# Four attentions with unnormalised weights, head pairs scaled by rows spread by way of DRAM, token sums in two steps

## The chip, the cores and the metric

One core of a Trainium2 chip runs the whole program. The metric is device time in microseconds from start to end of one execution; three runs of the kernel before are shown, and one more execution was profiled. TensorE multiplies matrices (weights are loaded into its array, the other operand streams through, results go to PSUM); VectorE and ScalarE work on tiles element by element and read PSUM and SBUF; GpSimd works on SBUF alone; SyncE only issues transfers (DMA). Each engine takes its own instructions in a fixed order and waits on semaphores for the others.

## The reference, cut to what matters

512 tokens (16 more, called meta, in the first block) of width 1024 pass one block and then two layers.

- First block: a forgetting attention (8 heads of 64; scores plus a decay bias, causal) and a latent attention (8 heads, queries and keys of 96, values of 64, mask by chunks). Each: `p = softmax(s); out = p @ v`, then times a gate `silu(...)`; both join into `@ w_out`, a norm and a residual.
- Each of the two layers: four branches on the same normed input, a recurrent one (mLSTM, 4 heads of 128), a grouped-query attention (8 heads of 64 on 2 key heads), a neighbourhood attention (8 heads of 64, on windows of keys with a bias table) and a differential attention (4 heads with values of 128); each branch's output goes through an up-projection times a gate, the sum through `w_out`, then a feed-forward part `(silu(h @ w_gate) * (h @ w_up)) @ w_down` of width 2816.

A softmax row may be normalised before or after the product with v: `(e / sum) @ v = (e @ v) / sum`. The four attentions with heads of 64 values (forgetting, latent, grouped-query, neighbourhood) are those that the change touches.

## The kernel before, in words

All products run in fp32r with operands split in a high and a low part (`evict_split`, L208, from PSUM; `split_w`, L217, for weights), and three products hi*hi, hi*lo, lo*hi (`mm3`, L248). Weights stream in tiles of 512 KB, three deep (`raw`, L226), issued by SyncE and split by ScalarE (high) and GpSimd or VectorE (low) into tiles three deep.

TensorE's order is the program's (`manual_schedule`, L671). The order on the other engines and on SyncE's queue is written by the framework's planner, which simulates the program and takes what is ready first; after that it is fixed. Between the attentions' steps a stream of projections is run (`Stream`, L74; `overlap`, L129): each head and each tile of 128 queries is one map with four stages, score (0), transpose (1), product with v (2) and, for the last map of a pair, `done` (3). Scores run `look` maps ahead of the transposes; stages 2 and 3 follow the transposes by `lag` maps. The numbers stand in L33 to L37: forgetting attention 2 ahead, 2 and 3 behind; latent 3, 3 and 5; grouped-query 3, 3 and 4; neighbourhood 3, 2 and 4.

**Scores.** `softmax` (L330), `softmax_of_sum` (L338) and `softmax_banks` (L348) write exponentials to a tile `p`, sum them on the way and take the reciprocal; then the score stage multiplies `p` by it: L1019 (forgetting, VectorE), L1059 and L1061 (latent, ScalarE for odd and VectorE for even query tiles), L1696 (grouped-query) and L1779 (neighbourhood), both VectorE.

**Heads.** `Head.trans` (L416) transposes `p` by blocks of 128 on TensorE (L316) into a PSUM bank and splits it into `pth` and `ptl` (L211, L212). `Head.pv` (L438, every second query tile) multiplies with v. Its stationary operand holds v's high part in columns 0 to 63 and its low part in 64 to 127 (L453 to L455), so of a head's 512 tokens the result has 128 rows, of which row d and row d + 64 must be added. At the last tile ScalarE copies all 128 rows to SBUF (L458). `pair_out` (L460) joins two heads: two transfers within SBUF move halves to the other 64 partitions (L464, L465), two VectorE adds (L466, L467) give a tile with one head in rows 0 to 63 and the other in 64 to 127. `done` multiplies it by the gate and splits it for the next product. Four pairs in each of the first block's attentions and four in each layer's two make 24.

**The feed-forward entry.** `ffn` (L1148) makes its first pair of gate and up tiles with plain products (`pair`, L1179), later pairs with a scheme of seven products (`fast_pair`, L582), which needs sums of quarters of the tokens and of the weights. `Tokens.sums` (L563) makes the token sums: for each half of the rows four differences (L571 to L574) and four splits (L576, L577). It is called between the two gates and the two ups of the first pair. Every second weight tile of the later pairs goes into tiles of the tag `qs` (L1150), in which the token quarters lie until the sums have read them. The weight sums are L599 to L602, their splits L591 and L592.

Tiles of one tag share a few buffers: `t2` has six (L319), `yn` (`gate_tile`, L525) three, PSUM's `A` eight banks.

Of the kernel before, what the change touches and what calls it, by code (L numbers as in the profile page):

```python
# [14 lines left out]
ALU = mybir.AluOpType  # L15
# [3 lines left out]
P = 128  # L19
# [146 lines left out]
def hybrid_kernel(ctx: ExitStack, tc: tile.TileContext, i: dict, out: bass.AP):  # L166
# [162 lines left out]

    def softmax(src, dst):  # L330

        st = new(small, [P, 3], "sm")
        V.tensor_reduce(st[:, 0:1], src, AX.X, ALU.max, negate=True)
        A_.activation(dst, src, AF.Exp, bias=st[:, 0:1], accum_out=st[:, 1:2])
        V.reciprocal(st[:, 2:3], st[:, 1:2])
        return st[:, 1:2], st[:, 2:3]

    def softmax_of_sum(parts, dst, scale=-1.0):  # L338
# [6 lines left out]
        V.reciprocal(st[:, 3:4], st[:, 2:3])  # L345
        return st[:, 2:3], st[:, 3:4]

    def softmax_banks(parts, dst):  # L348

        if len(parts) == 1:  # L350
            return softmax(parts[0][0], dst)[1]
# [7 lines left out]
        V.reciprocal(st[:, 5:6], st[:, 5:6])  # L359
        return st[:, 5:6]  # L360

# [46 lines left out]
    class Head:  # L408
# [3 lines left out]

        def __init__(self, v, blocks, meta=None):
            self.v, self.blocks, self.meta, self.pt, self.pm = v, blocks, meta, {}, {}

        def trans(self, t, p, col):  # L416

            if t % 2 == 0:
                self.pt[t // 2] = [new(pool, [P, 4, 256], n, F32R) for n in ("pth", "ptl")]
                if self.meta:  # L420
                    k.pm_turn = 256 - k.pm_turn
                    self.pm[t // 2] = [a[:, k.pm_turn:k.pm_turn + 256] for a in k.pm]
            qs = slice((t % 2) * P, (t % 2 + 1) * P)
            bl = self.blocks(t)
            pt = bank()
            if self.meta:
                if t % 2 == 0:
                    self.pmt = bank()[0:NMETA, 0:256]
                transpose(self.pmt[:, qs], p[:, self.meta[1]:self.meta[1] + NMETA])
            for j, b in enumerate(bl):  # L430
                transpose(pt[:, j * P:(j + 1) * P], p[:, col(b):col(b) + P])
            src = pt[:, 0:len(bl) * P].rearrange("p (b q) -> p b q", q=P)
            sl = slice(bl[0], bl[-1] + 1)
            evict_split(src, *(a[:, sl, qs] for a in self.pt[t // 2]))
            if self.meta and t % 2:
                evict_split(self.pmt, *(a[0:NMETA] for a in self.pm[t // 2]))

        def pv(self, t):  # L438
# [17 lines left out]
            if t == 3:  # L456
                self.z = t2()
                A_.copy(self.z, self.ps)  # L458

    def pair_out(heads):  # L460

        a, b = (h.z for h in heads)
        e = t2()
        nc.sync.dma_start(e[0:64], a[64:128])  # L464
        nc.sync.dma_start(e[64:128], b[0:64])  # L465
        V.tensor_tensor(e[0:64], a[0:64], e[0:64], ALU.add)  # L466
        V.tensor_tensor(e[64:128], b[64:128], e[64:128], ALU.add)  # L467
        return e

# [87 lines left out]
    class Tokens:  # L557
# [5 lines left out]
        def sums(self):  # L563
# [5 lines left out]
            for c in (slice(0, 2), slice(2, 4)):  # L569
# [5 lines left out]
                for j in (1, 2, 0, 3):  # L575
                    A_.copy(self.t[j][0][:, c], t[j])  # L576
                    V.tensor_tensor(self.t[j][1][:, c], t[j], f(self.t[j][0][:, c]), ALU.subtract)  # L577

        def quarter(self, a, b):
# [148 lines left out]
def first_body(k, fb, col, hl):  # L728
# [75 lines left out]

    def head(hd, v, vm):
        return k.Head(lambda b: v[:, b, hd], lambda t: list(range(t + 1)), (vm[:, hd], 0))

# [197 lines left out]
    def fox_head(hd):  # L1005
        u, e = fox.units[hd // 2], hd % 2
        st = Work()
        hobj = head(hd, *fox.v)
        fox.heads[hd] = hobj

        def sc(t):
# [5 lines left out]

            r = k.softmax_of_sum([(sp, st.cb[:, a:b], a, b) for sp, a, b in sps], p)[1]
            V.tensor_scalar(p, p, r, None, ALU.mult)  # L1019
            if t == 3 and hd in (1, 3):  # L1020
# [4 lines left out]
        def done():  # L1025
            e = k.pair_out([fox.heads[hd - 1], fox.heads[hd]])
            V.scalar_tensor_tensor(e, e, 0.5, u.gate, ALU.mult, ALU.mult)
# [19 lines left out]
    def mla_head(hd):  # L1047
        u = mla.units[hd]
        hobj = head(hd, *mla.v)
        mla.heads[hd] = hobj  # L1050

        def sc(t):
# [3 lines left out]
            p = k.p_tile(n)  # L1056
            r = k.softmax_banks(sps, p)
            if t % 2:
                A_.activation(p, p, AF.Copy, bias=0.0, scale=r)  # L1059
            else:  # L1060
                V.tensor_scalar(p, p, r, None, ALU.mult)  # L1061
            if t == 3 and hd < 6:
# [7 lines left out]
        def done():  # L1070
            j = hd // 2
            e = k.pair_out([mla.heads[hd - 1], mla.heads[hd]])
            V.scalar_tensor_tensor(e, e, 0.5, gates[j], ALU.mult, ALU.mult)
# [74 lines left out]
def ffn(k, x, l, h, quarters, last):  # L1148
# [392 lines left out]
def pair_maps(k, j, head, score, out, unit=None, before=None):  # L1541

    heads = [head(2 * j + e) for e in range(2)]

    def one(e, t):
        st = Work()

        def sc():
            st.p, st.col = score(e, t)

        def done():
            out(k.pair_out(heads))

# [11 lines left out]
def branch_b(k, w):  # L1565
# [117 lines left out]
    def maps(before):  # L1683
        def pair(j):
            def head(hd):
                return k.Head(lambda b: br.v[:, b, hd // 4], lambda t: list(range(NT)))

            def score(e, t):
                hd = 2 * j + e
# [21 lines left out]
def branch_c(k, w):  # L1711
# [49 lines left out]
    def maps(before):  # L1761
        def pair(j):
            u = br.units[j]

            def head(hd):
                return k.Head(lambda b: br.v[:, b, hd], lambda t: list(range(C_LO[t] // P, C_HI[t] // P)))

            def score(e, t):
                a, b = C_LO[t], C_HI[t]
# [230 lines left out]
```

## Time and profile before

| what | value |
|---|---|
| median of 3 runs (lowest, highest) | 2564.12 us (2560.34, 2567.02) |
| profiled execution: its own time | 2570.03 us |
| its span, first to last instruction | 2568.2 us |
| TensorE busy | 2488.4 us, 97% |
| VectorE busy | 1602.7 us, 62% |
| ScalarE busy | 1329.6 us, 52% |
| GpSimd busy | 939.0 us, 37% |
| mean granted TensorE clock | 0.990 |
| HBM read and written | 230 and 6 MB, 92 GB/s |

In the profile's lines PE is TensorE, PEld its weight loads, DVE VectorE, ACT ScalarE, POOL GpSimd, SP SyncE; a q behind it is the engine's sequencer, which issues transfers. L12 is line 12 of the kernel; a helper's line stands for all its callers. A matmul's duration includes its way through the array and overlaps the next one's. "A <- B" means that A stood idle until B had ended.

### The profile page before, as it was taken

Reading aid. Unit: us, or ns where it says so; the run is one execution under the profiler, and the core shown is the slowest. Engines: PE = TensorE matmul, PEld = TensorE weight load, DVE = VectorE, ACT = ScalarE, POOL = GpSimd, SP = SyncE. Lnnn points to the kernel's source line nnn. Section 1 sums busy time; section 2 is a strip of 40 time slices with the busy share of each in tenths; the row PEclk is TensorE's granted clock in tenths of the full one; section 3 lists DMA queues with packets and bytes.
Section 4 is the critical chain, followed back from the end, with each engine's and each line's share of the span. In section 5 each row is a group of like instructions: output and inputs, shape, how many; then the busy total and the mean of one; then the engine's idle time right before and its main releaser. Section 6 shows DMA issues by size and latency. Waiting matters only on the chain. (4 is left out here: it accounts for less than half of the span.)

```text
span 2568.2 us, 39912 instructions
## 1 busy us (share of the span) xinstructions
PE 2488.4 (97%) x14358; PEld 2159.6 (84%) x14358; DVE 1602.7 (62%) x3521; ACT 1329.6 (52%) x2893; POOL 939.0 (37%) x834
## 2 busy tenths in 40 slices
PE   7999999999999999989999999999999999899998
PEld 7988788888888878779999888888878878799997
DVE  3577557769335354577888567584354464787886
ACT  4567646647445444354444467475354453554443
POOL 4453346542565544400000456424655534100002
PEclk9999999999999999999999999999999999999999
DMA  5552233221537332422333232214374334232232
GB/s 149 145 142 68 88 128 103 77 95 55 145 105 189 106 105 83 148 91 99 101 106 107 99 110 88 88 57 132 108 186 115 97 89 135 87 107 99 101 105 82
DMA packets 117750, 277.20 MB, mean 108 GB/s; under 512 B 15824, under 2 KB 37584, under 8 KB 117552
## 3 DMA queue, kind: packets, MB, share of 16 engines
q1 hardware_dynamic: 117552, 274.65, 35.4%
q8 instruction: 113, 1.85, 0.3%
q14 instruction: 85, 0.70, 0.1%
HBM read 230.26 MB, written 6.46 MB: 92 GB/s over the span
## 5 line engine op out<-in xcount | busy, mean ns | idle before, releaser
L223 POOL TENSOR_TENSOR wlo<-raw,whi 128x512 fp32r<-128x512 f32 (+4 forms) x481 | 617.4, 1286 | 622.9 <-ACT whi L221 598.8
L221 ACT CAST whi<-raw 128x512 fp32r<-128x512 f32 (+4 forms) x573 | 345.7, 605 | 513.5 <-PE A L251 331.8
L250 PE MATMUL A<-hi,whi 128*128 128x512 f32 (+2 forms) x1368 | 535.5, 391 | 0.7 <-ACT hi L211 0.7
L252 PE MATMUL A<-hi,wlo 128*128 128x512 f32 (+2 forms) x1368 | 515.5, 377 | 2.7 <-POOL wlo L223 2.7
L251 PE MATMUL A<-lo,whi 128*128 128x512 f32 (+2 forms) x1368 | 516.8, 378 | 0.1
L252 PEld LDWEIGHTS A<-hi,wlo 128*128 128x128 f32 x1368 | 258.4, 189 | 53.8 <-POOL wlo L223 3.5
L250 PEld LDWEIGHTS A<-hi,whi 128*128 128x128 f32 x1368 | 258.7, 189 | 37.9 <-ACT hi L211 0.8
L251 PEld LDWEIGHTS A<-lo,whi 128*128 128x128 f32 x1368 | 259.1, 189 | 37.1 <-DVE lo L212 0.3
L651 POOL TENSOR_TENSOR ptl<-raw,pth 128x512 fp32r<-128x512 f32 x20 | 26.0, 1320 | 605.7 <-ACT pth L650 605.7
L212 DVE TENSOR_TENSOR ptl<-A,pth 128x512 fp32r<-128x512 f32 (+3 forms) x256 | 148.9, 582 | 103.9 <-ACT pth L211 102.5
L316 PE MATMUL A<-ident,p 128*128 128x128 f32 (+3 forms) x1125 | 176.2, 279 | 22.9 <-DVE p L540 17.5
L250 PE MATMUL A<-v,whi 128*128 128x256 f32 x640 | 182.3, 285 | 10.7 <-ACT whi L591 10.7
L316 PEld LDWEIGHTS A<-ident,p 128*128 128x128 f32 (+3 forms) x1125 | 136.5, 140 | 62.1 <-DVE p L540 19.7
L252 PE MATMUL A<-v,wlo 128*128 128x256 f32 x640 | 181.9, 284 | 3.8 <-DVE wlo L592 3.8
L251 PE MATMUL A<-ks,whi 128*128 128x256 f32 x640 | 181.2, 283 | 0.0
L344 ACT ACTIVATE p<-p,sms 128x512 f32<-128x512 f32 (+6 forms) x160 | 100.6, 629 | 121.0 <-DVE sms L342 116.1
L211 ACT CAST pth<-A 128x512 fp32r<-128x512 f32 (+3 forms) x256 | 128.0, 500 | 65.8 <-PE A L316 64.3
L223 DVE TENSOR_TENSOR wlo<-raw,whi 128x512 fp32r<-128x512 f32 x92 | 67.0, 728 | 125.4 <-ACT whi L221 125.2
L298 PE MATMUL A<-whi,hi 128*128 128x256 f32 (+7 forms) x440 | 144.5, 328 | 0.0
L300 PE MATMUL A<-whi,lo 128*128 128x256 f32 (+7 forms) x440 | 141.7, 322 | 0.0
L299 PE MATMUL A<-wlo,hi 128*128 128x256 f32 (+7 forms) x440 | 141.6, 322 | 0.0
L250 PEld LDWEIGHTS A<-v,whi 128*128 128x128 f32 x640 | 122.4, 191 | 17.2 <-ACT whi L591 11.2
(433 smaller groups left out, 6172.7 us busy)
## 6 DMA issues: line engine op xcount, KB each, us to landing
raw<-in_t_gl_dram SPq DMA_DIRECT2D x64, 512.0 KB, 3.5
raw<-in_w_ffn_down_dram SPq DMA_DIRECT2D x44, 512.0 KB, 3.6
raw<-in_w_in_dram SPq DMA_DIRECT2D x26, 512.0 KB, 3.5
raw<-in_w_out_dram SPq DMA_DIRECT2D x24, 512.0 KB, 3.6
raw<-in_t_gate_dram SPq DMA_DIRECT2D x24, 512.0 KB, 3.6
raw<-in_t_up_dram SPq DMA_DIRECT2D x24, 512.0 KB, 3.5
qs<-in_t_gate_dram SPq DMA_DIRECT2D x20, 512.0 KB, 4.4
qs<-in_t_up_dram SPq DMA_DIRECT2D x20, 512.0 KB, 4.2
```

The source lines that it names most:

```text
L211: A_.copy(hi, ps)
L212: V.tensor_tensor(lo, ps, f(hi), ALU.subtract)
L221: A_.copy(hi, src)
L223: (V if k.lo and k.turn % k.lo == 0 else G).tensor_tensor(lo, src, f(hi), ALU.subtract)
L250: T_.matmul(ps, sh, mh, start=first, stop=False, **kw)
L251: T_.matmul(ps, sh, ml, start=False, stop=False, **kw)
L252: T_.matmul(ps, sl, mh, start=False, stop=last, **kw)
L298: T_.matmul(ps, sh, wh[:, j], start=(b + j == 0), stop=False)
L299: T_.matmul(ps, sh, wl[:, j], start=False, stop=False)
L300: T_.matmul(ps, sl, wh[:, j], start=False, stop=(b + j == nk - 1))
L316: T_.transpose(dst, src, ident[0:k, 0:k])
L344: A_.activation(dst, dst, AF.Exp, bias=st[:, e:e + 1], scale=-1.0, accum_out=st[:, 2:3])
```

## The change

Four edits.

1. The weights `p` stay exponentials. The reciprocals go to a tile of 8 columns per pair (`Head.sums`: four query tiles of each head).
2. When the second head's last tile has been transposed, `spread` transposes that tile on TensorE to 8 rows of 128, copies them to SBUF, writes them to DRAM (4 KB), and reads them back as two rows of 512, each spread over 64 partitions; `done` multiplies the pair's output by that tile (`out`).
3. A head's halves are joined at its last product: ScalarE copies one half from PSUM to the pair's tile, at the partitions where the head belongs, and VectorE adds the other half from PSUM. The transfers of `pair_out` are gone.
4. `Tokens.sums` yields after each half; the first half is called after the first gate, the second after the second gate. The two gates go to `yn` tiles instead of `t2`.

```diff
-    def softmax(src, dst):
+    def softmax(src, dst, inv=None):
...
-        V.reciprocal(st[:, 2:3], st[:, 1:2])
-        return st[:, 1:2], st[:, 2:3]
+        inv = st[:, 2:3] if inv is None else inv
+        V.reciprocal(inv, st[:, 1:2])
+        return st[:, 1:2], inv
...
+        def __init__(self, v, blocks, meta=None, mate=None):
+            self.v, self.blocks, self.meta, self.pt, self.pm, self.mate = v, blocks, meta, {}, {}, mate
+            self.sums = mate.sums if mate else new(small, [P, 2 * NT], "inv")
+
+        def inv(self, t):
+
+            a = t + (NT if self.mate else 0)
+            return self.sums[:, a:a + 1]
+
+        def spread(self):
+
+            ps, rows = bank()[0:2 * NT, 0:P], new(small, [2 * NT, P], "invt", bufs=2)
+            transpose(ps, self.sums)
+            V.tensor_copy(rows, ps)
+            d, self.scale = rows_out(rows, "irows"), t2()
+            for e in range(2):
+                nc.sync.dma_start(self.scale[64 * e:64 * e + 64], d[NT * e:NT * e + NT].rearrange("t q -> (t q)").partition_broadcast(64))
+
+        def out(self):
+            V.tensor_tensor(self.e, self.e, self.scale, ALU.mult)
+            return self.e
...
+            if self.mate and t == NT - 1:
+                self.spread()
...
             if t == 3:
-                self.z = t2()
-                A_.copy(self.z, self.ps)
-
-    def pair_out(heads):
-
-        a, b = (h.z for h in heads)
-        e = t2()
-        nc.sync.dma_start(e[0:64], a[64:128])
-        nc.sync.dma_start(e[64:128], b[0:64])
-        V.tensor_tensor(e[0:64], a[0:64], e[0:64], ALU.add)
-        V.tensor_tensor(e[64:128], b[64:128], e[64:128], ALU.add)
-        return e
+
+                self.e = self.mate.e if self.mate else t2()
+                own, other = (slice(64, P), slice(0, 64)) if self.mate else (slice(0, 64), slice(64, P))
+                A_.copy(self.e[own], self.ps[other])
+                V.tensor_tensor(self.e[own], self.ps[own], self.e[own], ALU.add)
...
                 for j in (1, 2, 0, 3):
                     A_.copy(self.t[j][0][:, c], t[j])
                     V.tensor_tensor(self.t[j][1][:, c], t[j], f(self.t[j][0][:, c]), ALU.subtract)
+                yield
...
-            r = k.softmax_of_sum([(sp, st.cb[:, a:b], a, b) for sp, a, b in sps], p)[1]
-            V.tensor_scalar(p, p, r, None, ALU.mult)
+            k.softmax_of_sum([(sp, st.cb[:, a:b], a, b) for sp, a, b in sps], p, inv=hobj.inv(t))
...
-            r = k.softmax_banks(sps, p)
-            if t % 2:
-                A_.activation(p, p, AF.Copy, bias=0.0, scale=r)
-            else:
-                V.tensor_scalar(p, p, r, None, ALU.mult)
+            k.softmax_banks(sps, p, hobj.inv(t))
...
-            gts, us = [k.silu2(plain(gw), k.t2()) for _ in range(2)], []
-            tok.sums()
+            gts, us, sums = [], [], tok.sums()
+            for _ in range(2):
+                gts.append(k.silu2(plain(gw), k.gate_tile()))
+                next(sums)
...
-                r = k.softmax(sp, p)[1]
-                V.tensor_scalar(p, p, r, None, ALU.mult)
+                k.softmax(sp, p, inv)
...
-                r = k.softmax_of_sum([(sp, bias, 0, n)], p)[1]
-                V.tensor_scalar(p, p, r, None, ALU.mult)
+                k.softmax_of_sum([(sp, bias, 0, n)], p, inv=inv)
```

The other lines hand the pair's first head to the second one (`mate`) and call `heads[1].out()` where `pair_out(heads)` stood.

## Rows read from the trace of the kernel before

**Rows 1.** The page, first part: busy us (share of the span) x instructions.

```profile
PE 2488.4 (97%) x14358; PEld 2159.6 (84%) x14358; DVE 1602.7 (62%) x3521; ACT 1329.6 (52%) x2893; POOL 939.0 (37%) x834
```

**Rows 2.** Who TensorE waited for: us in total, times, longest us.

```profile
PE A L316 <- DVE p L540: 17.5, 7, 7.3
PE A L250 <- ACT whi L591: 10.7, 2, 5.5
PE A L455 <- DVE ptl L212: 6.8, 4, 2.4
...
PE A L252 <- DVE wlo L592: 3.8, 2, 2.0
PE A L316 <- ACT p L1059: 2.7, 2, 1.6
...
PE A L815 <- DVE v L212: 2.3, 1, 2.3
```

**Rows 3.** Windows: start:end length, busy us per engine, granted clock, DMA share, GB/s.

```profile
180.30:187.10 6.80, 6.01 (x24) 4.77 (x25) 5.48 (x19) 3.48 (x9) 2.57 (x2) 0.50 0.20 58
211.00:217.80 6.80, 5.06 (x17) 4.68 (x18) 5.09 (x14) 2.08 (x6) 1.26 (x1) 0.50 0.00 0
...
1129.20:1136.00 6.80, 3.65 (x15) 3.35 (x16) 6.76 (x11) 2.19 (x5) 0.00 (x0) 0.50 0.23 77
...
1927.90:1931.30 3.40, 3.40 (x13) 2.71 (x11) 2.33 (x7) 2.40 (x5) 1.87 (x2) 0.50 0.09 28
...
2238.60:2245.30 6.70, 4.25 (x18) 3.96 (x19) 6.67 (x11) 2.55 (x5) 0.00 (x0) 0.50 0.22 82
```

**Rows 4.** Timeline of VectorE, first feed-forward entry: start, us, instruction [idle before <- releaser].

```profile
1106.27 0.69 DVE L366 SCALAR_TENSOR_TENSOR t<-t,A 128x512 f32<-128x512 f32 x1 [2.45 <-ACT t L365]
...
1111.66 1.22 DVE L598 TENSOR_TENSOR ptl<-raw,pth 128x1024 fp32r<-128x1024 f32 x1 [4.01 <-ACT pth L597]
...
1114.00 0.68 DVE L571 TENSOR_TENSOR t<-qs,qs 128x512 f32<-128x512 f32 x1
...
1120.71 0.68 DVE L571 TENSOR_TENSOR t<-qs,qs 128x512 f32<-128x512 f32 x1
```

**Rows 5.** Timelines of SyncE and of TensorE in the same stretch.

```profile
1121.47 0.33 SPq L242 DMA_DIRECT2D qs<-in_t_gate_dram  x1
...
1130.31 0.58 PE L250 MATMUL A<-v,whi 128*128 128x256 f32 x1 [5.25 <-ACT whi L591]
```

**Rows 6.** Groups by line and shape; the last is L1696 in 560 to 680 us.

```profile
L1696 DVE TENSOR_SCALAR p<-p,sm 128x512 f32<-128x512 f32 x64 | 35.4, 559 | 0.9
...
L601 DVE TENSOR_TENSOR p<-raw,qs 128x512 f32<-128x512 f32 x40 | 27.6, 690 | 1.2
...
L466 DVE TENSOR_TENSOR t<-t,t 64x512 f32<-64x512 f32 x24 | 21.2, 883 | 32.9 <-DMA t<-t 32.9
...
L1696 DVE TENSOR_SCALAR p<-p,sm x32: 462/486/1293, 581.8 to 644.0; 128x512 f32<-128x512 f32 x32
```

**Rows 7.** Timelines at three pairs' joins: VectorE's adds, and TensorE at the first.

```profile
179.31 1.03 DVE L466 TENSOR_TENSOR t<-t,t 64x512 f32<-64x512 f32 x1 [0.96 <-DMA t<-t]
...
181.09 0.58 PE L455 MATMUL A<-ptl,v 128*64 128x256 f32 x2 [2.24 <-DVE ptl L212]
...
209.04 0.68 DVE L466 TENSOR_TENSOR t<-t,t 64x512 f32<-64x512 f32 x1 [2.34 <-DMA t<-t]
...
1925.38 1.56 DVE L466 TENSOR_TENSOR t<-t,t 64x512 f32<-64x512 f32 x1 [0.72 <-DMA t<-t]
```

**Rows 8.** Transposes with 36 columns; SyncE's timeline; landing of the reads of L1014 (264 KB).

```profile
L316 PE MATMUL A<-ident,p 128*36 128x128 f32 x16 | 2.1, 272 | 0.0
...
391.21 0.32 SPq L379 DMA_DIRECT2D arows<-arow  x1
...
392.99 1.28 SPq L1471 DMA_DIRECT2D cst<-arows  x3
...
DMA to landing us min/median/max: 3.2/4.1/4.7
```

More of the change, by code (lines that the diff above doesn't have):

```diff
@@ L334, in softmax, with softmax_of_sum @@
         A_.activation(dst, src, AF.Exp, bias=st[:, 0:1], accum_out=st[:, 1:2])
-        V.reciprocal(st[:, 2:3], st[:, 1:2])
-        return st[:, 1:2], st[:, 2:3]
-    def softmax_of_sum(parts, dst, scale=-1.0):
+        inv = st[:, 2:3] if inv is None else inv
+        V.reciprocal(inv, st[:, 1:2])
+        return st[:, 1:2], inv
+    def softmax_of_sum(parts, dst, scale=-1.0, inv=None):
         st = new(small, [P, 4], "sms")
@@ L344, in softmax_of_sum, with softmax_banks @@
         A_.activation(dst, dst, AF.Exp, bias=st[:, e:e + 1], scale=-1.0, accum_out=st[:, 2:3])
-        V.reciprocal(st[:, 3:4], st[:, 2:3])
-        return st[:, 2:3], st[:, 3:4]
-    def softmax_banks(parts, dst):
+        inv = st[:, 3:4] if inv is None else inv
+        V.reciprocal(inv, st[:, 2:3])
+        return st[:, 2:3], inv
+    def softmax_banks(parts, dst, inv):
         if len(parts) == 1:
-            return softmax(parts[0][0], dst)[1]
+            softmax(parts[0][0], dst, inv)
+            return
         st = new(small, [P, 6], "smb")
@@ L358, in softmax_banks @@
         V.tensor_tensor(st[:, 5:6], st[:, 3:4], st[:, 4:5], ALU.add)
-        V.reciprocal(st[:, 5:6], st[:, 5:6])
-        return st[:, 5:6]
+        V.reciprocal(inv, st[:, 5:6])
     def silu2(src, g):
@@ L408, in hybrid_kernel @@
     class Head:
-        def __init__(self, v, blocks, meta=None):
-            self.v, self.blocks, self.meta, self.pt, self.pm = v, blocks, meta, {}, {}
+        def __init__(self, v, blocks, meta=None, mate=None):
[14 more added lines that the diff above has]
+            return self.e
         def trans(self, t, p, col):
@@ L803, in v_tiles, with head @@
         return v.rearrange("p t h e d -> p t h (e d)"), vm.rearrange("p h e d -> p h (e d)"), put
-    def head(hd, v, vm):
-        return k.Head(lambda b: v[:, b, hd], lambda t: list(range(t + 1)), (vm[:, hd], 0))
+    def head(hd, v, vm, heads):
+        return k.Head(lambda b: v[:, b, hd], lambda t: list(range(t + 1)), (vm[:, hd], 0), heads[hd - 1] if hd % 2 else None)
     def scores(t, pairs, mask):
@@ L1007, in fox_head @@
         st = Work()
-        hobj = head(hd, *fox.v)
-        fox.heads[hd] = hobj
+        hobj = fox.heads[hd] = head(hd, *fox.v, fox.heads)
         def sc(t):
@@ L1025, in done @@
         def done():
-            e = k.pair_out([fox.heads[hd - 1], fox.heads[hd]])
+            e = hobj.out()
             V.scalar_tensor_tensor(e, e, 0.5, u.gate, ALU.mult, ALU.mult)
@@ L1048, in mla_head @@
         u = mla.units[hd]
-        hobj = head(hd, *mla.v)
-        mla.heads[hd] = hobj
+        hobj = mla.heads[hd] = head(hd, *mla.v, mla.heads)
         def sc(t):
@@ L1071, in done @@
             j = hd // 2
-            e = k.pair_out([mla.heads[hd - 1], mla.heads[hd]])
+            e = hobj.out()
             V.scalar_tensor_tensor(e, e, 0.5, gates[j], ALU.mult, ALU.mult)
@@ L1541, in pair_maps @@
 def pair_maps(k, j, head, score, out, unit=None, before=None):
-    heads = [head(2 * j + e) for e in range(2)]
+    heads = [head(2 * j, None)]
+    heads.append(head(2 * j + 1, heads[0]))
     def one(e, t):
@@ L1548, in sc @@
         def sc():
-            st.p, st.col = score(e, t)
+            st.p, st.col = score(e, t, heads[e].inv(t))
         def done():
-            out(k.pair_out(heads))
+            out(heads[1].out())
         needs = []
@@ L1684, in pair, with head, score @@
         def pair(j):
-            def head(hd):
-                return k.Head(lambda b: br.v[:, b, hd // 4], lambda t: list(range(NT)))
-            def score(e, t):
+            def head(hd, mate):
+                return k.Head(lambda b: br.v[:, b, hd // 4], lambda t: list(range(NT)), None, mate)
+            def score(e, t, inv):
                 hd = 2 * j + e
@@ L1763, in pair, with head, score @@
             u = br.units[j]
-            def head(hd):
-                return k.Head(lambda b: br.v[:, b, hd], lambda t: list(range(C_LO[t] // P, C_HI[t] // P)))
-            def score(e, t):
+            def head(hd, mate):
+                return k.Head(lambda b: br.v[:, b, hd], lambda t: list(range(C_LO[t] // P, C_HI[t] // P)), None, mate)
+            def score(e, t, inv):
                 a, b = C_LO[t], C_HI[t]
```

## Prediction, made before the changed kernel was built or run

> **What bounds the kernel now.** I read the page's first part, then who waited for whom on TensorE, then windows of the granted clock, then the timelines around the largest waits. The first part shows one engine that is nearly full: TensorE is busy 97% of the span [rows 1]. Work taken off VectorE, ScalarE or a queue therefore shortens nothing by itself; only TensorE's idle time, or its time at a low clock, can be won. The waits say where the idle time lies [rows 2]. The largest entry (L540, norm tiles) has nothing to do with the diff. The next ones have: the entry of both feed-forward parts (L591, L592), low halves of transposed weights that come late (ptl, L212), the end of the latent attention (L1059), and the passage from the first attention to the second (L815). The windows show a second cost: from these waits on TensorE is granted 0.50 of its clock, its lower level of 1.2 GHz, for some 3.4 or 6.8 us [rows 3]. So a wait costs itself and half of the busy time in such a stretch.
>
> **The sum's base.** The profiled execution took 2570.0 us, 0.23% above the median of the runs shown, 2564.1. Terms are worked out on the former and taken off the latter. About 0.3%, 7.7 us, is what a measurement of this kernel can tell from no change.
>
> **Token sums in two steps.** At the first feed-forward entry VectorE does all eight differences and eight splits in one run that starts at 1114.0, yet between the first gate's SiLU, done at 1107.0, and L598 it sat idle 4.0 us [rows 4]. The second half of the sums reaches its first difference (L571) at 1120.7. That instruction frees a tile into which gate weights go: their transfer is issued at 1121.5, sums of weights and the split L591 follow, and TensorE, idle 5.25 us, goes on at 1130.3 [rows 5]. From difference to product: 9.6 us. In the change the first half is emitted behind the first gate. A half takes 1120.7 - 1114.0 = 6.7 us, other work between included, so it fits between 1107.0 and 1113.7, and the second half starts near 1114. The product could then go at 1114 + 9.6 = 1123.6; TensorE gets there at 1130.3 - 5.25 = 1125.1. Cover of 1.5 us, so the wait should go almost wholly. Both layers: waits of 10.7 + 3.8 = 14.5 [rows 2], and two low-clock stretches in which TensorE was busy 3.65 and 4.25 us, half of it lost: 3.9 [rows 3]. Together 18.4; I take **16**, leaving a microsecond per layer. If the planner leaves the differences where they were, it is 0, the other bound. The first gates move to a tag of three tiles; a later output asks for two of these, but only after L1196 of the first pair has read them, so I cost that at nothing; without that cover it would be a wait like L591's, at most 5.25. The earlier differences also stand ahead of weight splits of the plain products on VectorE and ScalarE; three split tiles hide that, and the microsecond left over is for where they don't.
>
> **Weights unnormalised.** From VectorE go 64 multiplies at L1696, 35.4 us [rows 6], as many at L1779 and 48 shorter ones at L1019 and L1061; from ScalarE, 16 at L1059. This is load, not path: scores run two or three maps ahead of their transposes. It is path where that lead ends, at the end of the latent attention: L1059 held TensorE for 2.7 us [rows 2]; its transposes now follow the exponentials directly. I take **2**. The reciprocals stay.
>
> **Head halves joined.** Now each pair makes two 128 KB transfers behind the copies of L458, and VectorE stands in its fixed order at L466 until the first has landed: 32.9 us in 13 of 24 pairs [rows 6]. Queued behind that are the ptl halves that TensorE wants. Before 179.3 it idles 0.96 us and then adds for 1.03; TensorE waits 2.24 us until 181.1 [rows 7]. Before 1925.4 it idles 0.72 and adds for 1.56 [rows 7], and TensorE's longest wait for ptl, 2.4, is there. The change has ScalarE copy one half per head and VectorE add to it straight from PSUM, without a transfer: 48 adds as before, at the SBUF adds' 0.88 [rows 6] or less, and 0.69 for a row that has the SBUF to itself. Forgetting attention, third pair: 2.24 and half of 6.01 busy [rows 3], 5.2; I take **5**. Neighbourhood attention, third pair: the four ptl waits make 6.8 [rows 2]; without the 2.24 above and a short one in the latent attention I count 3.8 for both layers, and half of 3.4 at the low clock in the second [rows 3], 5.5. A multiply of 0.69 stands where 2.3 stood, so I take **3**. End of the forgetting attention: VectorE waits 2.34 for the join [rows 7], evictions of the next attention stand behind it, and TensorE loses 2.3 [rows 2] and half of 5.06 [rows 3], 4.8. The spread rows come about 1 us earlier than the join did and an add leaves the chain: I take **2**.
>
> **Rows spread by way of DRAM.** Added for each of 24 pairs: a transpose with eight columns as weights, a copy of 8x128, a 4 KB write, two reads of 128 KB, a multiply of 128x512. The transposes are TensorE's own: 16 of the nearest kind, with 36 columns, keep it busy 2.1 us, 0.13 each in a row, 0.27 alone [rows 8]. 24 of them cost 3.1, at most 6.5; I take **3**. The multiply has two SBUF inputs, 0.69 by L601 [rows 6]: 17 us in all, half of what L1696 alone gives back. The round trip: a row tile written at 391.21 is read from 392.99 on, 1.78 us, and a spread read of twice the size lands after 3.2 to 4.7 us, 4.1 at the median [rows 8]. With an issue and the copy the multiply can start 5.5 to 7 us after the transpose. Between the two lie three to five maps. Tightest is the grouped-query attention: 32 maps in 62.2 us [rows 6], 2.0 each, four of them, 8 us. The cover is 1 us there. If it goes, VectorE stands, and ptl behind it is late next. SyncE gets 24 more issues, and at each pair its reads stand about 1.8 us for the row, with weight loads behind them; three weight tiles hide that. For small new waits I put **1**, with bounds of 0 and 30.
>
> The Trainium skill, "DMA: Bandwidth & Descriptors", section "Anatomy of one DMA", gives about 2.0 us fixed plus bytes over 436 GB/s per transfer and calls the write receipt of DRAM the long part. By that the round trip would be an estimated 4.3 us, the end of the forgetting attention would give all of its 4.8, and the sum would be 3 lower; the base stays with the rows, 1.78 and 4.1.
>
> **Sum.** 16 + 2 + 5 + 3 + 2 - 3 - 1 = 24. 2564.1 - 24 = **2540** (2546 against the profiled execution).
>
> **Rivals.** (a) The feed-forward wait stays. The order on VectorE is the planner's; if it leaves the second half's first difference at 1120, the change doesn't do there what it says. For it: from 1114.0 to 1120.7 VectorE was already full of this work, and the freed tile, not the sums, starts the chain. Against: the idle 4.0 us ahead of it. Then 24 - 16 = 8: 2556. Chance 0.18. (b) All named waits and their low-clock stretches go: 18.4 + 2.7 + 5.2 + 5.5 + 4.8 - 3.1 = 33.5: 2531, or less where small waits that I have not counted go too. For it: each has the join or a multiply just ahead. Chance 0.16. (c) Slower: in the grouped-query attention the spread rows land after the multiply's turn. It decides from a round trip of 8 us on. Each of eight pairs would then cost what such a stand cost at the forgetting attention's third pair, 5.2: 42 us, 2540 + 42 = 2582. For it: SyncE must wait for the row, and its queue may stand at a weight load. Against: 5.5 to 7 us by the rows, and VectorE has eight multiplies less per pair to do before its turn. Chance 0.09. By the skill's figure this one could hardly happen.
>
> **Numbers.** The forecast has 0.57, its own range 2532 to 2552: all of the attention terms, or half of them and half of the feed-forward's doubt. Faster by over 0.3% (below 2556.4): 0.57, 0.16 and a third of (a): 0.78. Within 0.3%: the rest of (a): 0.13. Slower: (c), 0.09. The range reaches from full success and a little more, 2522, to (a) with some new waits, 2562; (c) is left out.
>
> **What would show it.** Right: no wait at L591 and L592, and a granted clock of 1.00, at the feed-forward entries; the first differences ahead of the second gate; no wait for ptl at the third pairs; 24 more transposes; VectorE over 50 us less busy. Wrong: L591 still among the waits; VectorE's new multiply waiting longer in total than the join's 32.9 us; new low-clock stretches in the grouped-query attention.

## The result, and the profile after

| | before | changed |
|---|---|---|
| median of 4 runs each | 2564.77 us | 2537.56 us (2536.44 to 2538.53) |
| ratio, 95% interval | 1 | 0.9896 (0.9879 to 0.9913) |
| profiled execution: own time; span | 2570.03; 2568.2 us | 2536.44; 2534.7 us |
| mean granted TensorE clock | 0.990 | 0.997 |

Faster by 1.0%, 27 us at the median; 2540 was forecast. The two profiled executions lie 33.6 us apart, because the one of before was 5 us above its median and the one after 1 us below. What these two traces say of the change is therefore some 6 us too good.

The first part of the changed kernel's page (busy us, share of the span, instructions):

```profile
PE 2475.9 (98%) x14382; PEld 2150.5 (85%) x14382; DVE 1526.7 (60%) x3393; ACT 1326.3 (52%) x2877; POOL 935.5 (37%) x834
```

Beside [rows 1], VectorE has 76 us less to do and TensorE 24 instructions more, yet TensorE is busy 12.5 us less. The reason is its clock. Of the stretches at half clock (ten before, five of them in [rows 3]) two are left, neither at a join nor at a feed-forward entry. Windows of them (start:end length, busy us per engine, granted clock, DMA share, GB/s):

```profile
336.10:342.90 6.80, 4.67 (x22) 4.66 (x23) 5.57 (x12) 3.00 (x9) 1.36 (x3) 0.50 0.38 139
957.30:960.70 3.40, 3.40 (x12) 2.71 (x11) 2.23 (x8) 1.93 (x5) 0.87 (x2) 0.50 0.60 134
```

Who TensorE waited for (us in total, times, longest):

```profile
PE A L316 <- DVE p L557: 17.5, 5, 8.2
...
PE A L252 <- DVE wlo L610: 2.1, 2, 1.1
...
PE A L250 <- DVE t L641: 1.4, 2, 0.7
...
PE A L479 <- DVE ptl L212: 0.4, 2, 0.2
```

The reader sees [rows 2] again with L591 (now L608) and L1059 gone, ptl down from 6.8 to 0.4, and two small waits per layer at the feed-forward entry in their place. VectorE's timeline there (start, us, instruction):

```profile
1092.19 0.69 DVE L588 TENSOR_TENSOR t<-qs,qs 128x512 f32<-128x512 f32 x1
1094.69 0.69 DVE L368 SCALAR_TENSOR_TENSOR yn<-t,A 128x512 f32<-128x512 f32 x1 [1.81 <-ACT t L367]
...
1100.71 0.68 DVE L588 TENSOR_TENSOR t<-qs,qs 128x512 f32<-128x512 f32 x1
...
1104.86 0.67 DVE L368 SCALAR_TENSOR_TENSOR yn<-t,A 128x512 f32<-128x512 f32 x1
...
1114.32 1.88 DVE L610 TENSOR_TENSOR wlo<-p,whi 128x512 fp32r<-128x512 f32 x3
```

The first differences (L588) stand even ahead of the first gate's SiLU (L368), the second half's ahead of the second gate's. In [rows 4] both followed both gates; the second gate's SiLU stood there:

```profile
1113.40 0.68 DVE L366 SCALAR_TENSOR_TENSOR t<-t,A 128x512 f32<-128x512 f32 x1
```

The new groups (busy us, mean ns of one, idle before them):

```profile
L485 DVE TENSOR_TENSOR t<-A,t 64x512 f32<-64x512 f32 x48 | 33.0, 688 | 43.0 <-ACT t L484 42.9
...
L435 DVE TENSOR_TENSOR t<-t,t 128x512 f32<-128x512 f32 x24 | 17.3, 722 | 10.0 <-DMA t<-irows 9.9
L429 DVE COPY invt<-A 8x128 f32<-8x128 f32 x24 | 6.6, 274 | 24.8 <-PE A L316 24.8
```

VectorE's stand for a transfer has fallen from 32.9 us in 13 pairs [rows 6] to 9.9 in 7. The 42.9 us behind ScalarE's half (L484) did not make the ptl halves late: TensorE's waits for them at these products are down to 0.4 us.

**One sum for every run.** As an estimate, the span is TensorE's full-speed work, plus half of its busy time at half clock, plus its idle time. The page gives the busy time; idle is the span less that; windows of the half-clock stretches (without the one in which each span ends) give the loss. It splits a gain by cause:

| profiled execution | span | idle | stretches at 0.50, us | lost to them | work at full speed |
|---|---|---|---|---|---|
| before | 2568.2 | 79.8 | 48.1 | 19.5 | 2468.9 |
| changed | 2534.7 | 58.8 | 10.2 | 4.0 | 2471.9 |
| e1_sums_alone | 2550.3 | 71.5 | 17.1 | 7.6 | 2471.2 |
| e3_join_alone | 2551.8 | 74.5 | 27.4 | 9.7 | 2467.6 |
| e4_spread_alone | 2575.0 | 85.6 | 51.3 | 20.2 | 2469.2 |
| e6_double | 2547.3 | 63.9 | 17.0 | 8.2 | 2475.2 |
| e9_join_and_sums | 2533.3 | 61.0 | 6.8 | 3.4 | 2468.9 |
| e10_changed_again | 2542.0 | 61.9 | 17.0 | 8.5 | 2471.6 |
| e11 (changed, GpSimd) | 2547.5 | 67.1 | 17.0 | 8.0 | 2472.4 |
| e12 (e9, GpSimd) | 2539.4 | 66.4 | 6.8 | 3.4 | 2469.6 |

Before to changed: 21.0 us less idle, 15.5 less lost to the clock, 3.0 more work, 33.5 in all. Nearly half of what these two executions show came back through the clock, and part of that is luck. At the third pair of the forgetting attention TensorE waits 2.24 us in the kernel before and 2.23 us in e1, which leaves the join as it was; the one execution was granted 0.50 from 180.3 us on, the other full clock. The changed kernel itself has 10.2 us at half clock in one execution and 17.1 in the other (e10). The last column scatters by 1 to 2 us between like kernels.

### The profile page after: what moved, and what is told of

It is laid out like the page before. It is cut to its first block, busy times and chain, and to the rows that moved or that the text cites. A ratio compares the mean times of both kernels' runs of the same rounds, so it can differ in the third digit from the quotient of the medians.

```text
span 2534.7 us, 39949 instructions
## 1 busy us (share of the span) xinstructions
PE 2475.9 (98%) x14382; PEld 2150.5 (85%) x14382; DVE 1526.7 (60%) x3393; ACT 1326.3 (52%) x2877; POOL 935.5 (37%) x834
## 4 chain that ended last, share of the span: by engine, by line
PE 73%; DVE 5%; DMA 2%; issue 2%; POOL 2%; ACT 1%; SPq 0%; DVEq 0%; POOLq 0%; ACTq 0%
PE A L250 16%; PE A L251 16%; PE A L252 16%; PE A L298 4%; PE A L300 4%; PE A L299 4%; PE A L316 4%; PE A L479 2%; PE A L517 1%; DVE x L1302 1%; DMA raw<-in_w_out_dram 1%; PE A L280 1%; PE A L518 1%; PE A L1708 1%; PE A L1707 1%
## 5 line engine op out<-in xcount | busy, mean ns | idle before, releaser
L251 PE MATMUL A<-ks,whi 128*128 128x256 f32 x640 | 179.7, 281 | 0.0
L211 ACT CAST pth<-A 128x512 fp32r<-128x512 f32 (+3 forms) x256 | 128.0, 501 | 65.9 <-PE A L316 63.9
L609 ACT CAST whi<-p 128x512 fp32r<-128x512 f32 x160 | 98.9, 622 | 62.8 <-PE A L251 56.9
```

What stands on the lines that cost most here:

```text
L211: A_.copy(hi, ps)
L251: T_.matmul(ps, sh, ml, start=False, stop=False, **kw)
```

## The experiments

My theory was the prediction's: the token sums and the join win, the spread rows cost a little. The rivals: the sums' gain comes from the gates' new tiles; the unnormalised weights are what wins; the join by itself wins nothing. The kernel before was timed again beside each group: 2568.61 us beside e1, e2, e7 and e8, 2568.79 beside e3 to e6, 2572.09 beside e9 to e12. Ratios are to these; the kernels that are compared by their medians ran in one group.

### The token sums, alone and taken back

e1 puts edit 4 on the kernel before; e2 takes it back from the changed kernel.

```diff
-            gts, us = [k.silu2(plain(gw), k.t2()) for _ in range(2)], []
-            tok.sums()
+            gts, us, sums = [], [], tok.sums()
+            for _ in range(2):
+                gts.append(k.silu2(plain(gw), k.gate_tile()))
+                next(sums)
...
                     V.tensor_tensor(self.t[j][1][:, c], t[j], f(self.t[j][0][:, c]), ALU.subtract)
+                yield
```

> The kernel before with the token sums in two steps and the two gates on yn tiles; nothing else changed. My theory (the feed-forward wait is a chain from the second half's first difference by way of the freed weight tile, and it is 6 to 8 us per layer): the waits at L591 and L592 go from 14.5 us to under 4, no low-clock stretch at either feed-forward entry, 2564.8 - 14 = 2551 us. Rival (VectorE, which is full there, only hands the wait to another product): waits of other lines in the same stretch take its place, 2560 us or more.

> The changed kernel with the token sums back in one step behind the second gate and the gates back on t2 tiles. My theory (the parts add up): the two entries wait as before, 14.5 us and two low-clock stretches, 2537.6 + 14 = 2551.5 us. Rival (in the changed kernel VectorE has less to do, so that the wait would have shrunk without the two steps): 2545 us or less.

e1: 2556.28 us, ratio 0.9944 (0.9928 to 0.9961), a gain of 14 us by the ratio. e2: 2556.08, 0.9945 (0.9925 to 0.9965); against the changed kernel's 0.9896 the part is worth 0.0049, some 13 us. Alone or last, it gives nearly the same. Waits of TensorE in e1:

```profile
PE A L455 <- DVE ptl L212: 7.9, 6, 2.2
...
PE A L252 <- DVE wlo L593: 2.4, 3, 1.1
...
PE A L250 <- DVE t L624: 1.4, 2, 0.7
```

and in e2:

```profile
PE A L250 <- ACT whi L608: 10.5, 2, 5.3
...
PE A L252 <- DVE wlo L609: 4.7, 4, 2.0
```

In e1 the wait of 10.7 us is gone and ptl stays; in e2 the reverse, and the clock falls to 0.50 at both entries again. The traces can also be matched product by product: TensorE's order is the program's, so each of its instructions in the kernel before has a partner in another run, and the lead of one over the other can be read at any place. By that the two entries win 13.1 us in e1 and 13.5 in the changed kernel.

### Which of the edit's two changes does it

e7 keeps the gates on the new tiles but emits the sums behind both gates; e8 keeps the two steps but leaves the gates on `t2`.

```diff
# e7
             for _ in range(2):
                 gts.append(k.silu2(plain(gw), k.gate_tile()))
+            for _ in range(2):
                 next(sums)
# e8
-                gts.append(k.silu2(plain(gw), k.gate_tile()))
+                gts.append(k.silu2(plain(gw), k.t2()))
```

> The changed kernel, gates on yn tiles, but all token sums emitted behind the second gate. My theory (the place of the first half decides): nearly the time of the kernel with the sums undone, 2551 us, first difference behind the second gate. Rival (the planner was held back by the gates' t2 tiles alone; once these are gone it takes the differences early wherever they are written): 2538 us, first difference ahead of the first or second gate.

> The changed kernel with the sums in two steps but both gates on t2 tiles. My theory (the two steps do it, the tiles nothing): 2538 us, waits at the entries as in the changed kernel, about 1.8 us per layer. Rival (six t2 tiles for two gates, two temporaries and eight differences hold the second half back): part of the wait returns, 2543 to 2551 us.

e7: 2558.0, 0.9952 (0.9937 to 0.9968): all of the part's gain is lost. e8: 2544.82, 0.9906 (0.9888 to 0.9924): nearly all of it stays. One row of e7's waits shows the old wait back:

```profile
PE A L250 <- ACT whi L609: 9.3, 2, 4.6
```

VectorE's timeline in e7 shows why:

```profile
1098.92 0.68 DVE L588 TENSOR_TENSOR t<-qs,qs 128x512 f32<-128x512 f32 x1
...
1106.19 0.68 DVE L368 SCALAR_TENSOR_TENSOR yn<-t,A 128x512 f32<-128x512 f32 x1
...
1110.24 0.68 DVE L588 TENSOR_TENSOR t<-qs,qs 128x512 f32<-128x512 f32 x1
```

The planner does move differences: the first half's first one stands 7.3 us ahead of the second gate's SiLU, though e7's program writes it behind. That wins nothing, because the second half's first difference is still 4.1 us behind that gate, and TensorE goes on 10.8 us after it (9.6 in the kernel before). So the place of the second half decides. My theory for e7 (the first half's place) and its rival (the planner takes the differences early, and the time comes with them) are each wrong in one half. In e8 the second half's first difference stands directly behind the second gate, 0.6 us after its start, and one wait of 1.5 us is left in each layer:

```profile
PE A L252 <- DVE wlo L610: 3.4, 3, 1.5
```

By the ratios the tiles are worth 0.001, which lies within the intervals. By the traces the two entries win 11.0 us in e8 against 13.5, with 0.50 granted behind both of those waits, so that "the tiles nothing" is not shown. Rival (a) of the prediction falls by the changed kernel's own trace: there the second half's first difference stands ahead of the second gate.

### The join alone

e3 is the kernel before with edit 3: halves joined from PSUM, weights normalised in place, sums in one step.

```diff
-                self.z = t2()
-                A_.copy(self.z, self.ps)
+                self.e = self.mate.e if self.mate else t2()
+                own, other = (slice(64, P), slice(0, 64)) if self.mate else (slice(0, 64), slice(64, P))
+                A_.copy(self.e[own], self.ps[other])
+                V.tensor_tensor(self.e[own], self.ps[own], self.e[own], ALU.add)
...
     def out(self):
         return self.e
```

> The kernel before with head halves joined from PSUM (a copy and an add per head, no transfers), weights normalised in place as before, no spread rows, sums in one step. My theory (VectorE's stand for the join's transfers makes the ptl halves late): no wait for ptl at the third pairs of the forgetting and the neighbourhood attention, the passage between the first two attentions shorter, 9 to 10 us less, 2555 us. Rival (the multiplies' load makes ptl late): those waits stay, 2562 us or more.

2554.16, 0.9952 (0.9936 to 0.9968): 12 us. Its waits:

```profile
PE A L250 <- ACT whi L605: 10.4, 2, 5.3
PE A L515 <- DVE ptl L212: 6.6, 6, 1.4
...
PE A L316 <- ACT p L1071: 3.1, 3, 1.5
```

The wait for ptl at the product that `Head.pv` makes is no longer among its largest; L515 is the product with v of heads with values of 128, which no edit touches (6.6 us in the kernel before too). The half-clock stretches at 180, 211 and 1928 us [rows 3] are gone, but e1, with the old join, has none near 180 and 1928 either, so it is the waits that show the cause, not the clock. Matched with the kernel before, e3 wins 5.9 us at the end of the forgetting attention (203 to 222 us there). What is left is what the join does not touch: the feed-forward entry, and ScalarE's normalising at the end of the latent attention.

### The unnormalised weights and the spread alone

e4 has edits 1 and 2, with the halves still joined by transfers.

```diff
-            V.tensor_tensor(self.e, self.e, self.scale, ALU.mult)
-            return self.e
+            a, b, e = self.mate.z, self.z, t2()
+            nc.sync.dma_start(e[0:64], a[64:128])
+            nc.sync.dma_start(e[64:128], b[0:64])
+            V.tensor_tensor(e[0:64], a[0:64], e[0:64], ALU.add)
+            V.tensor_tensor(e[64:128], b[64:128], e[64:128], ALU.add)
+            V.tensor_tensor(e, e, self.scale, ALU.mult)
+            return e
```

> The kernel before with unnormalised weights and spread rows, the pair joined by transfers and two adds as before and then multiplied, sums in one step. My theory: VectorE still stands at the join, so the ptl waits at the third pairs stay in part; the latent attention's end gains 2 to 3 us, 24 transposes cost 3, a longer tail costs some: 2563 us, between 2559 and 2568. Rival (the multiplies' load was the cause): the ptl waits go, 2555 us.

2572.1, 1.0005 (0.9994 to 1.0016): nothing. VectorE has 64 us less to do than before (1538.3), and the join's transfers hold it longer than the 32.9 us of [rows 6]:

```profile
DVE t L438 <- DMA t<-t: 45.8, 15, 8.7
```

### The spread's cover, and its price

e5 issues the spread where the pair's last product ends, not where its last tile has been transposed. e6 does transpose, copy and round trip twice per pair (the second result is used, the first is not).

```diff
# e5
-            if self.mate and t == NT - 1:
-                self.spread()
...
                 V.tensor_tensor(self.e[own], self.ps[own], self.e[own], ALU.add)
+                if self.mate:
+                    self.spread()
# e6
             if self.mate and t == NT - 1:
                 self.spread()
+                self.spread()
```

> The changed kernel with the sums' rows transposed, written and spread when the pair's last product with v is issued, two or three maps later than now. My theory (the cover of the round trip is one to a few microseconds): VectorE's waits for the spread rows rise from 9.9 us to some 70 (24 times 3), some of it reaches TensorE: 2545 to 2555 us, most of it at the grouped-query and latent attentions. Rival (the round trip is hidden with room to spare): 2538 us.

> The changed kernel with the spread done twice for each pair: a second transpose, copy, write and two reads, of which the second set is used. My theory (the transposes are all of the price): TensorE busy by 3.1 us more, 2541 us. Rival (the transfers and the queue have a price of their own): 2545 us or more, with weight loads or the multiply late.

e5: 2552.01, 0.9937 (0.9923 to 0.9950), about 10 us behind the changed kernel by the ratios. VectorE's stand:

```profile
DVE t L435 <- DMA t<-irows: 50.9, 23, 6.7
```

That is 23 of 24 pairs, where the changed kernel stood in 7, and half clock is back at 182, 212 and 291 us. So the three to five maps of cover are what keeps the spread from costing more, as the prediction argued. e6: 2550.38, 0.9933 (0.9918 to 0.9947), about 9 us. Here the stand hardly grew:

```profile
DVE t L435 <- DMA t<-irows: 11.6, 8, 2.8
```

TensorE's work rose by 3.3 us (the table), the transposes' own cost, and my theory that this is all falls; the rest is idle time and half clock, which I could not pin on single waits. The second spread also takes one more of the six `t2` tiles, and VectorE stood 1.3 us at L985 until a read into such a tile had landed, so the 9 us are not shown to be the price of the transfers alone.

### Join and sums without the spread

If a second spread costs 9 us, the first may cost more than it brings. e9 is e3 with the two-step sums: edits 3 and 4, weights normalised as before. e10 is the changed kernel again, on the same chip.

```diff
             k.softmax_of_sum([(sp, bias, 0, n)], p, inv=inv)
+            V.tensor_scalar(p, p, inv, None, ALU.mult)
...
-            if self.mate and t == NT - 1:
-                self.spread()
...
     def out(self):
-        V.tensor_tensor(self.e, self.e, self.scale, ALU.mult)
         return self.e
```

> The kernel before with the two-step token sums (and the gates on y tiles) and the join of the halves from PSUM; the attention weights are normalised in place as before, and there are no transposes of sums, no DRAM round trip and no final multiply. Ratios to the kernel before, on the same chip as the changed kernel. Theory: the join and the sums make the whole gain, the unnormalised weights with their spread rows nothing: 0.9896 as the product of the two single parts' ratios (0.9944 times 0.9952), within 0.0012 of the changed kernel on this chip, with the wait for the latent attention's fourth map (3.1 us, transpose behind ScalarE's normalising) still there and TensorE's 24 extra transposes (3 us) gone. Rival 1: the unnormalised weights do save the 2 to 5 us that the prediction gave them: 0.9912 to 0.992, behind the changed kernel by 4 to 6 us. Rival 2: the spread costs more than it gives, as doubling it cost some 9 us: ahead of the changed kernel by 4 to 9 us, 0.987.

> The changed kernel, without an edit, on the chip of the other three, to compare them with it directly: 0.9896 of the kernel before, the interval of its first timing being 0.9879 to 0.9913.

e9: 2535.67 us (2535.06 to 2540.38), ratio 0.9863 (0.9842 to 0.9883). e10: 2542.46 (2539.66 to 2544.59), 0.9883 (0.9865 to 0.9902). The version without the spread is ahead by 6.8 us at the median: my theory of "nothing" falls, rival 2 holds. The intervals overlap and one run of e9 lies among those of e10; but e12 and e11 below are the same pair of kernels with one more edit, and lie 7.9 us apart the same way. First part of e9's page:

```profile
PE 2472.3 (98%) x14358; PEld 2145.6 (85%) x14358; DVE 1600.2 (63%) x3521; ACT 1336.2 (53%) x2893; POOL 937.6 (37%) x834
```

VectorE does 73 us more than in the changed kernel, and the program is faster. One row of its waits is the one that the unnormalised weights were to save:

```profile
PE A L316 <- ACT p L1072: 3.0, 3, 1.5
```

Where do the 8.7 us between the two profiled executions come from? By the table: 2.7 work, 0.9 idle, 5.1 half clock. Matched instruction by instruction, e9 is 1.2 us behind e10 at 170 us and 6.4 ahead at 218: the second half of the forgetting attention and its end. TensorE's waits in 165 to 225 us of e10:

```profile
PE A L479 <- DVE yl L212: 2.8, 1, 2.8
PE A L250 <- DVE t L984: 1.6, 1, 1.6
PE A L833 <- ACT sth L214: 0.6, 1, 0.6
PE A L833 <- DVE stl L215: 0.6, 1, 0.6
```

and of e9:

```profile
PE A L830 <- DVE sms L343: 1.1, 1, 1.1
PE A L476 <- DVE yl L212: 0.6, 1, 0.6
```

Behind e10's first two waits stands VectorE, and behind VectorE the spread. VectorE's timeline at the last pair:

```profile
196.02 0.28 DVE L429 COPY invt<-A 8x128 f32<-8x128 f32 x1 [0.42 <-PE A L316]
...
204.25 0.69 DVE L435 TENSOR_TENSOR t<-t,t 128x512 f32<-128x512 f32 x1 [4.23 <-DMA t<-irows]
204.97 1.14 DVE L984 TENSOR_TENSOR t<-A,rope 128x64 f32<-128x64 f32 x8
```

From copy to multiply it is 8.2 us, 4.2 of them a stand; directly behind is L984, for which TensorE waits 1.6. SyncE's waits in 190 to 203 us tell why it is late:

```profile
SPq L432 <- DMA irows<-invt: 2.4, 1, 2.4
```

SyncE stood 2.4 us for the 4 KB row to be written, and the first read was issued 3.5 us after the write. At the third pair VectorE stood 1.6 us at its multiply; the split of yl behind it came late, and TensorE waited 2.8. In the first profile of the same kernel the last pair's read followed its write by 1.3 us, VectorE stood 1.9 there and not at all at the third pair, and TensorE's wait for yl was 0.8. The remaining stretches of e10 at half clock (342, 571, 1868 and 2059 us) follow waits for a norm tile (L557), for a query tile (L1670), for a transfer of the neighbourhood attention (at L1789) and for ptl at L518. None of these lines is part of the change, though that transfer goes through the same queue of SyncE as the spread's; why this execution had more of them than e9's stays open.

One place tells the same in every profile. Matched with the kernel before, the end of the forgetting attention (203 to 222 us there) wins 5.9 us in each of e3, e9 and e12, which have the join without the spread. In the six executions with this spread it wins 3.8 where VectorE stood 1.9 us at the last pair's multiply (the changed kernel), 1.3 where it stood 2.1 to 2.7 (e2, e7, e8), 0.7 at 3.6 (e11) and 0.05 at 4.2 (e10). So 2 to 6 us of the spread's price are paid there, more the later the rows land. The end of the latent attention (265 to 300 us) wins 2.7 in all six and 1.8 in those three: beside the join the unnormalised weights are worth 0.9 us.

### VectorE's last load at the entry, moved to GpSimd

Two waits per layer are left at the feed-forward entry, both for VectorE, while GpSimd has three splits to do there, 4.6 us in all. e11 is the changed kernel, and e12 is e9, with half of the low parts on GpSimd:

```diff
-                    V.tensor_tensor(self.t[j][1][:, c], t[j], f(self.t[j][0][:, c]), ALU.subtract)
+                    (G if j in (0, 3) else V).tensor_tensor(self.t[j][1][:, c], t[j], f(self.t[j][0][:, c]), ALU.subtract)
```

> The changed kernel with half of the low parts of the token sums (of t0 and t3, four subtractions a layer, 0.68 us each on VectorE) on GpSimd, which is idle from 1106 us on. Theory (VectorE alone is late at the start of the feed-forward): the two waits left there, 1.1 us for a split at L610 and 0.7 us for the add at L641, go in both layers, 3.5 us: 2540 less 3.5 where the changed kernel has 2540, ratio to it 0.9986. Rival: GpSimd's subtraction lengthens VectorE's operations beside it, or TensorE waits for GpSimd's low part (1.3 us each) of t3 or t0: the same or up to 3 us slower.

> The first kernel of this call (join and two-step sums, weights normalised in place) with the same four low parts a layer on GpSimd. Theory: both effects add: the first kernel's time less 3.5 us, and as fast as or faster than the changed kernel with that edit. Rival: as told there, no gain from GpSimd.

e11: 2550.5 (2546.77 to 2554.11), 0.9917 (0.9900 to 0.9934), 8.0 us behind e10. e12: 2542.57, 0.9890 (0.9872 to 0.9909), 6.9 behind e9. My theory falls and the rival holds, though it had put the loss at 3 us at most. GpSimd's timeline in e11:

```profile
1099.35 1.40 POOL L594 TENSOR_TENSOR ks<-t,v 128x512 fp32r<-128x512 f32 x1 [0.30 <-ACT v L593]
...
1104.40 1.56 POOL L594 TENSOR_TENSOR ks<-t,v 128x512 fp32r<-128x512 f32 x1 [1.95 <-ACT v L593]
```

and VectorE's beside it:

```profile
1098.81 0.78 DVE L589 TENSOR_TENSOR t<-cst,t 128x512 f32<-128x512 f32 x1
1099.52 1.78 DVE L590 TENSOR_TENSOR t<-cst,qs 128x512 f32<-128x512 f32 x1
...
1102.93 0.68 DVE L591 TENSOR_TENSOR t<-cst,t 128x512 f32<-128x512 f32 x1
...
1104.73 1.78 DVE L588 TENSOR_TENSOR t<-qs,qs 128x512 f32<-128x512 f32 x1
```

Beside each of the four moved subtractions of this layer a VectorE operation takes 1.77 to 1.79 us, not 0.68: moving 0.68 costs 1.1. VectorE falls behind, and TensorE waits 2.6 us in each layer for a split of the plain products:

```profile
PE A L252 <- DVE wlo L223: 5.3, 2, 2.6
```

Matched as above, the two entries win 6.7 us in e11 and 7.1 in e12, where e10 and e9 win 13.5 and 13.6: that is most of the 8.0 and 6.9.

The Trainium skill, "SBUF — State Buffer", section "Who interferes with whom", says that a VectorE instruction with two SBUF inputs contends with a GpSimd instruction that reads SBUF. This trace agrees: 1.78 against 0.68 us for the same operation.

## Why the prediction was right, and where its steps were not

**The time** was right: 2540 against 2537.56, 24 us against 27, and so were the sign and the bound (one full engine, of which only idle time and low clock can be won). The split of the sum was not. (In its chances, a third of 0.18 is 0.06, so 0.79 and 0.12 should stand for 0.78 and 0.13.)

**Token sums, 16:** right in mechanism, measured at 12 to 14, and at 13.5 by the matched entries. The step that was a little off is the one that let "a microsecond per layer" stand: 1.1 and 0.7 us were left in each, 3.5 in both. The place was earlier than I worked out: I put the second half's first difference near where the first half's had been, directly behind the second gate, and it stood 4.2 us ahead of it.

**Join, 5 + 3 + 2 = 10:** measured at 12 by e3. The waits named were the right ones: ptl fell from 6.8 to 0.4 in the changed kernel. The sizes were not: the end of the forgetting attention, put at 2, wins 5.9 without the spread and 0.05 to 3.8 with it. The terms also took every half-clock stretch as the wait's own price, and e1 shows the same wait without one.

**Weights unnormalised, 2:** the wait did go, and it was worth 0.9. The step that failed is that a removed wait counts almost in full. From 255 us to the end of that attention e9 waits 3.6 us, 2.8 of them for L1072; e10, without that wait, still waits 2.8, mostly for ptl, for yl and for the exponentials themselves. In its first profile the changed kernel even gave 1.9 back directly behind, where TensorE's wait for a norm tile (L557) was 5.9 us and had been 4.0; in e10, the same kernel, it was 4.1 and nothing was given back. So this loss is of one execution.

**Rows spread, 3 + 1:** the transposes' 3 is what the work column shows (3.0, doubled 3.3). The 1 for small new waits was too small. Together with the unnormalised weights the net was put at -2, and measures 7 to 8 us slower beside the join and the sums (e10 less e9, e11 less e12). The step that failed is the one that took the row's write as 1.78 us, one case: the first read of the spread row (L432) follows the write's issue by 1.2 to 3.5 us, so that at the tightest joins the cover is gone in some executions. The cover was worked out for the grouped-query attention, as the tightest; the loss came at the end of the forgetting attention, which wins 2 to 6 us less with the spread than without. At two pairs of the neighbourhood attention the write itself was issued only 3.7 and 3.9 us after the copy. Where VectorE stood, its multiply came 5.5 to 10.1 us after the copy, against the 5.5 to 7 of the prediction. Its other estimate, 4.3 us, was further off: the section of the Trainium skill that it is taken from, "Anatomy of one DMA" in "DMA: Bandwidth & Descriptors", gives its figure for transfers that GpSimd issues, and here SyncE issues them. What the rest of the 7 to 8 us is made of stays open.

The cover at the grouped-query attention was right: the multiply came 6.7 to 9.5 us after the copy and stood 0.03 us at most, so rival (c) did not come true. Nor did VectorE stand longer in total than the 32.9 us that would have shown me wrong.

**Why the total held all the same:** the join and the sums together, put at 26, gave 35 of 2572 us in e9 (interval 30 to 41; the product of their single ratios makes it 27), and the weights with their spread took 7, not 2. Two errors of 5 to 9 us went against each other; that the total fell so near the forecast is luck. Rival (b)'s 33.5 is, to a tenth, the difference of the two profiled spans; that is chance, since the medians differ by 27.

## What to carry to other kernels

When one engine is full, write each execution as full-speed work, plus half-clock loss, plus idle time of that engine, and ask of each part of a change which of the three it moves: taking 73 us of load from VectorE moved none, while the 24 transposes that paid for it were work on the full engine. Try each part of a bundled change alone and try the bundle without it; here the best version has two of the four edits, 2535.67 against 2542.46 us. Before work goes to an idle engine, look for rows in which both engines already run side by side: in the changed kernel VectorE's L591 took 1.78 us at 1097.8 us, beside a split that GpSimd had begun at 1097.4, and 0.68 at 1108.3 with GpSimd at rest.

## What the runs showed of the hardware that I had not expected

- **Half clock follows small waits, though not each one, and not each time.** The wait at the forgetting attention's third pair, 2.24 us in the kernel before and 2.23 in e1, was met with 0.50 in the one and full clock in the other. In e10 TensorE waits 1.57, 0.46, 0.61 and 0.60 us within 204 to 211 us and is granted 0.50 from 212.6 on; its longer single wait of 2.8 us up to 179.7 is not followed by half clock. The feed-forward entry's 1.07 and 0.69 us in the changed kernel were followed by full clock in both layers, e8's single 1.5 us by 0.50 in both.
- **A 4 KB write can hold a queue for long.** SyncE stood 27.2 us in 20 of 24 pairs for the row to be written (30.9 in 21 in e10), and the read's issue followed the write's by 1.2 us at best and 3.5 at worst.
- **Two busy elementwise engines are not two.** A VectorE operation on two 128x512 SBUF tiles beside a GpSimd subtraction took 1.78 us instead of 0.68 (e11). The new wait for L1209 in the changed kernel (1.0 us) is of that kind: two of its splits, at 1413.7 and 1415.4 us, took 1.77 us each while GpSimd split weights.
